# A two-branch encoder layer on one core: attention products trimmed to the query rows that see the keys, exponentials in a slot of their own, first weights staged in idle buffers, and a reordered passage to the tail

## The chip, the core and the metric

The kernel runs on one core of one Trainium2 chip. Its engines work in parallel, each through its own queue in order: TensorE (PE; its weight loads are shown as PEld), VectorE (DVE), ScalarE (ACT), GpSimd (POOL), and SyncE (SP), which here issues all DMAs. The metric is the device time of one execution in microseconds. Before the change it is 2601.07 us, the median of three runs (2600.2 to 2602.27).

## The reference

Two groups of 2048 tokens (prompt and sample) pass through one layer with shared weights. Cut to what matters:

```python
h = rms_norm(x, norm_w)                                    # 1024 wide
q_a, k_a, v_a, g_a, q_b, k_b, v_b, g_b = split(h @ w_in)   # 512,128,128,512, 4 x 512
# A: 8 query heads on 2 key heads, keys within +-128 tokens, a sink per head
o_a = windowed_gqa_sink(rope(norm(q_a)), rope(norm(k_a)), v_a, sink_a) * silu(g_a)
# B: tokens as a grid of 32 rows x 64 columns; row r sees the 8 rows from clip(r - 4, 0, 24),
#    and 16 columns; a learned bias by distance; 8 heads of 64
o_b = neighbourhood_attn(norm(q_b), norm(k_b), v_b, rpb_b) * silu(g_b)
x = x + concat(o_a, o_b) @ w_out
x = x + (p @ w_ple) * sigmoid(x @ w_ple_gate)
```

## The kernel before, in words

Everything is fp32. Each operand of a product is held as a high part (`hi`) and a remainder (`lo`), and a product is three matmuls, hi x hi, hi x lo and lo x hi. A weight is split by `split_w`: ACT casts the high part (L148), DVE subtracts (L149). A tile of x is split by `split`: ACT casts (L295), POOL subtracts (L296). `mm` (L203) records a matmul, `tr` (L206) a transpose, which is a matmul against an identity matrix `ident`.

Work goes over tiles `f` of 128 tokens. **Stage A** takes tiles 0 to 31: per tile the projections `pk` (keys and values), `pq` (queries) and `pg` (gate) of branch A, and an attention unit of an earlier tile. **Stage B** takes tiles 32 to 95, that is each group twice, once for each half of the eight heads: `pqk` and `pvg` project, and a unit of attention works on a query block of 8 grid rows x 16 columns. Such a unit makes four score matrices (`scb`, 128 queries x up to 512 keys), adds the bias and takes the maximum on DVE, takes exponentials on ACT (L233, with the sums of rows in `den`; `nm`, the negated maximum, comes from DVE, L229), transposes them on PE in chunks of up to 128 keys (`ptb`, L206), copies them to `p_t` as hi (ACT, L735) and lo (DVE, L736), and multiplies with the values (`pob`, L203). One `pob` matmul takes a chunk of keys and streams 256 columns, 128 queries in hi and 128 in lo. A unit has 3 or 4 chunks and 4 heads, and there are 832 such matmuls. `fin` transposes the gate (`pgtb`) and multiplies.

PE's order is fixed by hand: a stream of projection matmuls, with pieces of the units set in at the places that the tables `PLAN_A` and `PLAN_B` give, as fractions of the tile's projections. `P(...)` pins an instruction of another engine to its place in the program; what is not pinned is moved by a scheduler. Weights that change between stages are loaded in pieces by jobs that a pump releases, or that `flush` runs by name.

**The head** (tiles 0 and 1) has no earlier tile to fill PE with. `load_first` (L188) brings two row blocks of weights at a time into a staging tile in one of the three `p_t` buffers, and splits them: `wx` for pk, `wa` (w_q) for pq, `wb` (w_g) for pg. Then PE takes pk of both tiles, pq of both and pg of both. pk, pq and pg share the PSUM buffers "pj" (3); score and transpose tiles use "sc" (3).

**The passage to the tail**: the last tiles of `out_ahead` multiply the finished attention outputs with w_out (`pout`), add x (`ev`, L844 to L846) and store. The tail then does the remaining output projection and the gate's by products of sums of blocks, seven products instead of eight for each group of 512 tokens. `load_q` (L952) loads the weight sums `s1` to `s4` (tiles `s`, `wb`), `load_raw` the attention outputs of one group (`oar`, L979, and `obr`, L980), and `prep(m)` makes the operand `opd` of product m (sums at L1009 to L1020, the cast at L995). The products are the matmuls `acca` and `accc` (L1043).

## Time and profile before

| | |
|---|---|
| median of three runs | 2601.07 us |
| the profiled execution | 2597.39 us |
| its span, from the first to the last instruction | 2595.6 us |
| mean granted TensorE clock in it | 0.993 |
| busy share PE / DVE / ACT / POOL | 98% / 75% / 54% / 30% |
| DMA traffic | 357.49 MB, mean 138 GB/s |

A row of a timeline gives the start in us from the span's beginning, the busy us, engine, line, operation, output <- inputs, the shape, how many instructions were merged into the row (x), and in brackets how long the engine stood idle before it and what ended that. PE is the engine that is nearly always busy; so what matters is where it waits and how long its instructions take from start to start, since matmuls overlap and their busy times add to more than they cost. SPq is the queue of SP, and its rows are the issuing of DMAs, not the transfers.

### The profile page before, as it was taken

The numbers are of one execution on the slowest core, as the hardware profiler recorded it, in microseconds if no ns is written. First come the engines' busy times: TensorE is split into PE (matmuls) and PEld (weight loads), VectorE is DVE, ScalarE is ACT, GpSimd is POOL, SyncE is SP. The second block draws the span as 40 slices with busy tenths as digits, with TensorE's granted clock in tenths as the row PEclk, the third lists the DMA queues.
The fourth block names the chain that finished last, engine by engine and source line by source line (L and its number), as shares of the span: only waits on it lengthen the run. The fifth ranks groups of instructions, "written<-read, shape, count | busy, mean of one in ns | idle before, by whom it ended". The sixth has DMA issues, their size and how long they took to land.

```text
span 2595.6 us, 47039 instructions
## 1 busy us (share of the span) xinstructions
PE 2538.2 (98%) x16080; PEld 2273.8 (88%) x16080; DVE 1938.8 (75%) x5702; ACT 1414.0 (54%) x3327; POOL 787.3 (30%) x996
## 2 busy tenths in 40 slices
PE   7999999999989999999999999999989999999999
PEld 5888888888877888888788888888989999999999
DVE  5888888888886888888888888888655648555454
ACT  5666666666664666666766666666432214222222
POOL 3332333332223333333233333321122323233321
PEclk9999999999999999999999999999999999999999
DMA  5333332111143554555654554456575455232221
GB/s 178 108 109 102 108 87 94 60 62 52 62 122 105 183 191 152 183 187 165 219 188 153 187 170 154 151 162 200 172 257 180 154 172 182 82 118 91 78 82 45
DMA packets 227518, 357.49 MB, mean 138 GB/s; under 512 B 37936, under 2 KB 115376, under 8 KB 222128
## 3 DMA queue, kind: packets, MB, share of 16 engines
q1 hardware_dynamic: 227280, 354.50, 42.7%
q8 instruction: 127, 2.08, 0.3%
q14 instruction: 111, 0.91, 0.1%
HBM read 266.33 MB, written 105.92 MB: 143 GB/s over the span
## 4 chain that ended last, share of the span: by engine, by line
PE 89%; DVE 5%; ACT 3%; DMA 2%; issue 1%; POOL 1%; SPq 0%; DVEq 0%; ACTq 0%; POOLq 0%
PE pqk L203 13%; PE pvg L203 12%; PE acca L1043 12%; PE accc L1043 9%; PE pg L203 6%; PE pq L203 6%; PE pob L203 4%; PE pple L203 3%; PE pout L203 3%; PE ptb L206 3%; PE scb L203 3%; PE sc L203 3%; PE pk L203 3%; PE po L203 3%; PE pt L206 3%
## 5 line engine op out<-in xcount | busy, mean ns | idle before, releaser
L233 ACT ACTIVATE s<-s,nm 128x384 f32<-128x384 f32 (+4 forms) x512 | 306.1, 600 | 311.3 <-DVE nm L229 185.0
L203 PE MATMUL pvg<-wb,xr 128*128 128x512 f32 x1536 | 456.7, 405 | 0.0
L203 PE MATMUL pqk<-wa,xr 128*128 128x512 f32 x1536 | 436.6, 407 | 0.0
L203 PEld LDWEIGHTS pqk<-wa,xr 128*128 128x128 f32 x1536 | 266.9, 189 | 37.0
L203 PEld LDWEIGHTS pvg<-wb,xr 128*128 128x128 f32 x1536 | 268.5, 189 | 31.7
L296 POOL TENSOR_TENSOR xr<-stx,xr 128x512 fp32r<-128x512 f32 x192 | 246.6, 1298 | 152.9 <-ACT xr L295 152.5
L203 PE MATMUL pg<-wb,xr 128*128 128x512 f32 x768 | 233.3, 411 | 3.6 <-DVE q L463 3.6
L203 PE MATMUL pq<-wa,xr 128*128 128x512 f32 x768 | 221.9, 402 | 4.1 <-ACT wa L148 2.5
L244 POOL TENSOR_TENSOR g<-qg,rd 128x256 f32<-128x256 f32 x64 | 39.5, 618 | 494.9 <-DVE rd L242 481.0
L1043 PE MATMUL acca<-opd,s 128*128 128x256 f32 x1344 | 166.0, 285 | 3.1 <-ACT r L1075 2.5
L1043 PEld LDWEIGHTS acca<-opd,s 128*128 128x128 f32 x1344 | 164.1, 193 | 3.8 <-ACT r L1075 2.7
L203 PEld LDWEIGHTS pq<-wa,xr 128*128 128x128 f32 x768 | 140.2, 190 | 28.3 <-ACT wa L148 3.0
L218 DVE CUSTOM_DVE_ANT_0 s<-scb,bias 128x288 f32<-128x288 f32 (+3 forms) x256 | 141.8, 555 | 29.1 <-PE scb L203 23.7
L203 PEld LDWEIGHTS pg<-wb,xr 128*128 128x128 f32 x768 | 138.7, 191 | 25.1 <-issue 4.0
L735 ACT CAST p_t<-ptb 96x384 fp32r<-96x384 f32 (+3 forms) x256 | 129.5, 508 | 52.8 <-PE ptb L206 50.9
L736 DVE TENSOR_TENSOR p_t<-ptb,p_t 96x384 fp32r<-96x384 f32 (+3 forms) x256 | 149.0, 584 | 8.2 <-ACT p_t L735 5.3
L616 ACT ACTIVATE ks_b<-pktb,wk 64x128 fp32r<-64x128 f32 x256 | 125.1, 489 | 49.3 <-DVE ks_b L617 41.6
L203 PEld LDWEIGHTS pob<-p_t,vw 128*128 128x128 f32 (+2 forms) x832 | 132.8, 190 | 20.7 <-DVE p_t L736 2.5
L617 DVE SCALAR_TENSOR_TENSOR ks_b<-pktb,wk,ks_b 64x128 fp32r<-64x128 f32 x256 | 115.1, 450 | 38.8 <-ACT ks_b L616 31.7
L203 PE MATMUL pob<-p_t,vw 128*128 128x256 f32 (+2 forms) x832 | 140.5, 282 | 2.0 <-DVE p_t L736 2.0
L1009 POOL TENSOR_TENSOR opd<-sum,opd 128x1024 fp32r<-128x1024 f32 x28 | 69.6, 2484 | 232.1 <-ACT opd L995 232.1
L576 DVE TENSOR_TENSOR pr<-pt,pr 128x512 fp32r<-128x512 f32 x184 | 125.5, 684 | 14.6 <-ACT pr L575 13.6
(197 smaller groups left out, 5870.3 us busy)
## 6 DMA issues: line engine op xcount, KB each, us to landing
stx<-x_b SPq DMA_DIRECT2D x128, 256.0 KB
vw<-v_d SPq DMA_DIRECT2D x112, 256.0 KB
stx<-x_a SPq DMA_DIRECT2D x64, 256.0 KB
stn<-x_n SPq DMA_DIRECT2D x64, 256.0 KB
v_d<-vb SPq DMA_DIRECT2D x64, 256.0 KB
x1r<-x_d SPq DMA_DIRECT2D x16, 1024.0 KB
y_t<-r SPq DMA_DIRECT2D x64, 256.0 KB
v_d<-vb SPq DMA_DIRECT2D x96, 128.0 KB
```

What stands on the lines that cost most here:

```text
L203: pinned(nc.tensor.matmul(out, lhsT, rhs, start=start, stop=stop))
L206: pinned(nc.tensor.transpose(out, in_, ident))
L218: nc.vector.tensor_tensor_reduce(out=s[:, :n], in0=ps[:, :n], in1=bias, scale=1.0, scalar=-3.0e38, op0=ALU.add, op1=ALU.max, accum_out=sm[ ...
L233: nc.scalar.activation(ss[i][:, :n], ss[i][:, :n], AF.Exp, bias=nm[:, i:i + 1], accum_out=den[:, i:i + 1])
L296: nc.gpsimd.tensor_tensor(out=lo, in0=raw, in1=hi.bitcast(F32), op=ALU.subtract)
L576: nc.vector.tensor_tensor(out=pr[:, 1], in0=pf, in1=pr[:, 0].bitcast(F32), op=ALU.subtract)
L616: nc.scalar.activation(hi, pkt[a:a + 64, i], AF.Copy, scale=wk[a:a + 64, 1:2])
L617: nc.vector.scalar_tensor_tensor(out=lo, in0=pkt[a:a + 64, i], scalar=wk[a:a + 64, 1:2], in1=hi.bitcast(F32), op0=ALU.mult, op1=ALU.subtract)
L735: nc.scalar.copy(p_t[:kc, :nch, 0], pf)
L736: nc.vector.tensor_tensor(out=p_t[:kc, :nch, 1], in0=pf, in1=p_t[:kc, :nch, 0].bitcast(F32), op=ALU.subtract)
L1009: each(lambda x, y, z: eng.tensor_tensor(out=x, in0=y, in1=z, op=ALU.subtract), out, a, b)
L1043: pinned(nc.tensor.matmul(ps[:, kk], w[k][:, a, c:c + 128], o[:, b, k], start=i in (0, 1, 4) and kk == 0 and k == 0 and j == 0, stop=k == ...
```

## The change

It has four parts.

1. **Trim.** A grid row of queries sees 8 rows of keys, so in a chunk of 4 or 5 rows of keys part of the 8 query rows see nothing and their probabilities are zero. `query_rows` gives the rows that see chunk j. The transposes go against a permuted identity (`rowwise`), so that the queries come out row by row; chunks are packed in `p_t` with the seen rows only; the `pob` matmuls run over these columns, the chunk with all the rows first. Of the 832 matmuls, 320 keep 256 columns, 256 have 128, 128 have 160 and 128 have 224. The copies to `p_t` shrink with them (128 x 512 to 128 x 368, 120 x 384 to 120 x 288, 384 to 320 or 304 in the others), and the output needs no rearranging in `fin`.
2. **Exponentials.** In stage B `nm` stays at the last score; the four exponentials get a slot of `PLAN_B` of their own (0.16), the first one pinned, in the order in which the transposes take them (0, 2, 1, 3).
3. **Head.** All first weights are loaded at once, into tiles that are idle then (`p_t`, `raw`, `qg`), and split later. The remainder of tile 0's x is made on DVE instead of POOL. pk of tiles 0 and 1 and pg of tile 1 use "sc" for PSUM. The gate splits are pinned behind the first pq. The transposes of tile 0's queries come after 18 of the matmuls of tile 1's pg. The first loads of later tiles come after the weights'.
4. **Passage.** The load of `oar` and `obr` comes ahead of the loads of s2, s1 and s3; the x tiles for the last `ev` are loaded ahead; the `ev` additions and the operands of products 0 to 13 are pinned; the weight jobs are flushed in three places instead of one.

The core of the diff:

```diff
+def query_rows(b, cb, j):
+    r0, _, _, _, rows = window(b, cb)
+    k0 = r0 + rows * j
+    see = [r for r in range(8) if k0 - 7 <= min(max(8 * b + r - 4, 0), 24) <= k0 + rows - 1]
+    return (see[0], max(see[-1] + 1, 4)) if see[0] == 0 else (min(see[0], 4), see[-1] + 1)
...
 PLAN_B = (
...
-    (0.24, 0, "fin", 0), (0.35, 1, "prep", 0),
+    (0.16, 1, "exp", 0), (0.24, 0, "fin", 0), (0.35, 1, "prep", 0),
...
+    nc.gpsimd.tensor_copy(rowwise.rearrange("p (r c) -> p r c", c=16), ident.rearrange("p (c r) -> p r c", r=8))
...
-        for i in range(4):
-            nc.scalar.activation(ss[i][:, :n], ss[i][:, :n], AF.Exp, bias=nm[:, i:i + 1],
-                                 accum_out=den[:, i:i + 1])
+        for n_, i in enumerate((0, 2, 1, 3) if sink is None else range(4)):
+            ex = nc.scalar.activation(ss[i][:, :n], ss[i][:, :n], AF.Exp, bias=nm[:, i:i + 1],
+                                      accum_out=den[:, i:i + 1])
+            if sink is None and n_ == 0:
+                P(ex)
...
+    st = [main.tile([128, 4, 256], F32, tag="p_t", name="ws", bufs=3) for _ in range(2)]
...
+    raws_q += load_first(main.tile([128, 2, 512], F32, tag="p_t", name="ws", bufs=3), 0, 256, 512)
+    raw = ap.tile([128, 4, 512], F32, tag="raw", name="ws", bufs=1)
+    raws_q += load_first(raw[:, 0:2], 2, 256, 512)
...
+        split(0, i, low=nc.vector)
+        for j in range(2 * i, 2 * i + 2):
+            split_w(wx[:, j], raws_x[j], nw[:, j:j + 1])
...
+    for j in (0, 2):
+        raws_g += load_first(main.tile([128, 2, 512], F32, tag="p_t", name="ws", bufs=3), j, 768, 512)
+    for j in range(4, KT):
+        raws_g += load_first(ap.tile([128, 1, 512], F32, tag="qg", name="wg", bufs=6), j, 768, 512)
...
-        pk = ptile([128, 256], "pj", "pk")
+        pk = ptile([128, 256], "pj" if f > 1 else "sc", "pk")
...
-        pg = ptile([128, 512], "pj", "pg")
+        pg = ptile([128, 512], "sc" if f == 1 else "pj", "pg")
...
+        sees = [query_rows(b, cb, j) for j in range(nch)]
+        order = sorted(range(nch), key=lambda j: sees[j][1] - sees[j][0])
+        at = [16 * sum(z - a for a, z in sees[:j]) for j in range(nch + 1)]
...
-            for j in range(nch):
-                tr(pt[:kc, 128 * j:128 * j + 128], sm["s"][h][:, kc * j:kc * j + kc])
+            for j in order:
+                c = at[j] - 16 * sees[j][0]
+                tr(pt[:kc, c:c + 128], sm["s"][h][:, kc * j:kc * j + kc], rowwise)
...
-            for j in range(nch):
-                mm(po[:, i, :], vw[j][:kc, h, :], p_ts[x][:kc, j].rearrange("p a q -> p (a q)"),
-                   j == 0, j == nch - 1)
+            for j in order[::-1]:
+                a, z = sees[j]
+                mm(po[:, i, :].rearrange("p (a q) -> p a q", a=2)[:, :, 16 * a:16 * z], vw[j][:kc, h, :],
+                   p_ts[x][:kc, :, at[j]:at[j + 1]], j == order[-1], j == order[0])
...
-            nc.vector.tensor_tensor(out=ev, in0=ps, in1=ev, op=ALU.add)
+            ev = evs[mp] if evs else load_ev(n, mp)
+            P(nc.vector.tensor_tensor(out=ev, in0=ps, in1=ev, op=ALU.add))
...
+            for j in range(KT // 2, KT):
+                split_w(w[j], raws[j], nw[:, j:j + 1])
+            drain(first[0], 23)
+            for j in range(KT):
+                split_w(w_g[j], raws_g[j], nw[:, j:j + 1], P)
+            drain(first[0], 1)
+            drain(first[1], 24)
+            continue
         for gen in first:
+            if count > 24 and gen is first[1]:
+                drain(gen, 18)
+                nxt(-1)
             drain(gen, count)
...
+        load_o(AHEAD - 1, False)
+        evs = [load_ev(AHEAD - 1, mp) for mp in range(3)]
         load_raw(0)
+        evs.append(load_ev(AHEAD - 1, 3))
+        LEAD = 2
+        ahead = out_ahead(AHEAD - 1, evs)
+        drain(ahead, 24)
+        for name in ("s2", "s1", "s3"):
+            ws[0][name] = load_q(0, name)
         for _ in range(3):
             load_x()
-        flush("0s3")
-        LEAD = 2
-        ahead = out_ahead(AHEAD - 1)
-        drain(ahead, 144)
+        drain(ahead, 120)
         prep(0)
+        flush("0s2")
         drain(ahead)
...
         prep(1)
+        flush("0s1")
...
-            if m == 4:
-                flush("0s4")
+            flush({0: "0s3", 4: "0s4"}.get(m))
```

The order in which the engines issue these things is best seen in three places. First SP's DMAs of the head (`stx` and `stn` are x and the normalised copy of it, `ws` and `wg` staged weights, 128x2x512 is two row blocks of w_q or w_g; `ev` is x for the tail). Before:

```order
L188 DMA ws<-w_in 128x2x256 x3
L278 DMA stx<-x_a 128x512 x2
L278 DMA stn<-x_n 128x512
L188 DMA ws<-w_in 128x2x256
L278 DMA stn<-x_n 128x512
L188 DMA ws<-w_in 128x2x512 x2
L278 DMA stn<-x_n 128x512 x2
L278 DMA stx<-x_a 128x512 x2
L351 DMA snk<-sink 128x8
L354 DMA cs<-rope 128x512
L356 DMA rw<-rope_w 128x64
L188 DMA ws<-w_in 128x2x512 x2
```

and now:

```order
L290 DMA stx<-x_a 128x512
L198 DMA ws<-w_in 128x2x256
L290 DMA stx<-x_a 128x512
L198 DMA ws<-w_in 128x2x256 x3
L290 DMA stx<-x_a 128x512 x2
L198 DMA ws<-w_in 128x2x512 x2
L290 DMA stn<-x_n 128x512 x2
L198 DMA ws<-w_in 128x2x512
L352 DMA cs<-rope 128x512
L354 DMA rw<-rope_w 128x64
L290 DMA stn<-x_n 128x512 x2
L198 DMA ws<-w_in 128x2x512
```

The third and fourth loads of w_q were the last row shown, behind the loads of the normalised x, of a later tile and of three small tables. Now the fourth is the last row shown, the third stands four rows ahead of it, and the loads of later tiles come after this piece.

Second, ACT at the change of halves in stage B (`wa` is the second half's weight, `s,den<-s,nm` the exponentials, `p_t<-ptb` the copy after the transposes; each line number of before has moved down by 11 to 36). Before:

```order
L148 ACTIVATE wa_16591<-wa_16591,nw 128x512
L295 CAST xr<-stx 128x512
L148 ACTIVATE wa_16593<-wa_16593,nw 128x512
L754 COPY otb<-pob 64x512
L148 ACTIVATE wa_16595<-wa_16595,nw 128x512
L148 ACTIVATE wa_16597<-wa_16597,nw 128x512
L148 ACTIVATE wa_16599<-wa_16599,nw 128x512
L689 CAST q1b<-pqtb 64x256
L233 ACTIVATE s,den<-s,nm 128x512 x4
L689 CAST q1b<-pqtb 64x256
L735 CAST p_t<-ptb 128x4x128
```

and now:

```order
L159 ACTIVATE wa_16590<-wa_16590,nw 128x512
L307 CAST xr<-stx 128x512
L159 ACTIVATE wa_16596<-wa_16596,nw 128x512
L790 COPY otb<-pob 64x512
L243 ACTIVATE s,den<-s,nm 128x512 x4
L159 ACTIVATE wa_16598<-wa_16598,nw 128x512
L159 ACTIVATE wa_16600<-wa_16600,nw 128x512
L159 ACTIVATE wa_16602<-wa_16602,nw 128x512
L718 CAST q1b<-pqtb 64x256
L771 CAST p_t<-ptb 128x368
```

Three of the weight casts that stood ahead of the exponentials stand behind them.

Third, DVE in the passage to the tail (`opd<-oar` is the remainder for product 0, `opd<-obr` for product 1, `sum` the sum for product 2, `s_...` the remainders of the weight sums). Before:

```order
L153 TENSOR_TENSOR s_24977<-s_24977 128x512
L153 TENSOR_TENSOR s_24979<-s_24979 128x512
L1009 TENSOR_TENSOR opd<-oar,opd 128x1024
L1009 TENSOR_TENSOR opd<-obr,opd 128x256 x4
L1012 TENSOR_TENSOR sum<-sum,oar 128x1024
L845 TENSOR_TENSOR ev<-pout,ev 128x512 x2
L1070 TENSOR_TENSOR r<-acca,xres 128x512 x2
```

and now:

```order
L1053 TENSOR_TENSOR opd<-oar,opd 128x1024
L164 TENSOR_TENSOR s_25027<-s_25027 128x512
L164 TENSOR_TENSOR s_25029<-s_25029 128x512
L164 TENSOR_TENSOR s_25031<-s_25031 128x512
L164 TENSOR_TENSOR s_25033<-s_25033 128x512
L882 TENSOR_TENSOR ev<-pout,ev 128x512 x2
L1053 TENSOR_TENSOR opd<-obr,opd 128x256 x4
L164 TENSOR_TENSOR s_25035<-s_25035 128x512
L164 TENSOR_TENSOR s_25037<-s_25037 128x512
L164 TENSOR_TENSOR s_25039<-s_25039 128x512
L164 TENSOR_TENSOR s_25041<-s_25041 128x512
L1056 TENSOR_TENSOR sum<-sum,oar 128x1024
```

The additions `ev`, which free the PSUM of `pout`, stood behind all of the first operands and are now ahead of `opd<-obr`; the remainders of the weight sums, which stood ahead of all of these, are spread between them. On SP, `oar` and `obr` stood behind the twelve loads `s<-sums` and are now ahead of them.

117 lines of the change are left out of this document (58 added, 59 removed).

## The prediction

> **What bounds the kernel now.** I read the page first, then busy time by stretches of the span, then PE's timeline wherever a stretch was not full, and at each hole the timeline of the engine that ended it. From the page:
>
> ```profile
> PE 2538.2 (98%) x16080; PEld 2273.8 (88%) x16080; DVE 1938.8 (75%) x5702; ACT 1414.0 (54%) x3327; POOL 787.3 (30%) x996
> PE 89%; DVE 5%; ACT 3%; DMA 2%; issue 1%; POOL 1%; SPq 0%; DVEq 0%; ACTq 0%; POOLq 0%
> ```
>
> PE is busy for 2538.2 of 2595.6 us and is 89% of the chain that ended last. So only two things can be won: matmul time, and the holes in PE's row. The stretches (window, its length, busy us of PE, PEld, DVE, ACT, POOL, the granted clock, DMA share, GB/s) say where the holes are:
>
> ```profile
> 0.00:51.45 51.45, 36.16 (x151) 28.81 (x152) 30.59 (x106) 25.88 (x51) 17.17 (x33) 0.93 0.56 179
> 800.00:1250.00 450.00, 449.55 (x2395) 377.65 (x2395) 357.21 (x1133) 280.17 (x662) 147.27 (x173) 1.00 0.55 175
> 1250.00:1285.00 35.00, 29.02 (x152) 22.68 (x152) 32.09 (x78) 28.61 (x60) 12.15 (x14) 1.00 0.70 224
> 1890.00:1935.00 45.00, 36.12 (x283) 35.36 (x282) 24.98 (x35) 15.10 (x27) 11.67 (x11) 0.92 0.78 261
> 1935.00:2595.60 660.60, 651.97 (x5411) 650.96 (x5410) 373.22 (x484) 182.84 (x275) 193.48 (x112) 1.00 0.36 122
> ```
>
> The steady part of stage B has no hole (449.55 of 450): there an edit counts only if it shortens matmuls. The head lacks 15.3 us of 51.45, the change of halves 6.0 of 35, the passage to the tail 8.9 of 45. The change touches all three.
>
> **The head (tiles 0 and 1).** PE's timeline, then ACT, DVE, SP and the stretch of densest transfers:
>
> ```profile
> 7.06 0.58 PE L203 MATMUL pk<-wx,xr 128*128 128x256 f32 x1 [7.06 <-ACT wx L148]
> 22.96 0.49 PE L203 MATMUL pq<-wa,xr 128*128 128x512 f32 x1 [2.52 <-ACT wa L148]
> 29.05 5.70 PE L203 MATMUL pq<-wa,xr 128*128 128x512 f32 x24 [0.43 <-DVE vr L430]
> 38.40 3.85 PE L203 MATMUL pg<-wb,xr 128*128 128x512 f32 x10 [3.65 <-DVE q L463]
> 51.45 0.76 PE L203 MATMUL pk<-wx,xr 128*128 128x256 f32 x5
> ...
> 4.47 0.62 ACT L295 CAST xr<-stx 128x512 fp32r<-128x512 f32 x1 [2.45 <-DMA stx<-x_a]
> 22.19 2.65 ACT L148 ACTIVATE wa<-ws,nw 128x512 fp32r<-128x512 f32 x4 [2.08 <-DMA ws<-w_in]
> ...
> 7.04 2.89 DVE L149 SCALAR_TENSOR_TENSOR wx<-ws,nw,wx 128x256 fp32r<-128x256 f32 x6 [3.41 <-ACT wx L148]
> 16.80 2.75 DVE L149 SCALAR_TENSOR_TENSOR wa<-ws,nw,wa 128x512 fp32r<-128x512 f32 x4 [2.11 <-ACT wa L148]
> 20.98 1.43 DVE L359 TENSOR_TENSOR tab<-cs,rw 128x256 f32<-128x256 f32 x4 [0.48 <-DMA rw<-rope_w]
> 23.02 0.17 DVE L127 TENSOR_SCALAR rqki<-vr 128x3 int32<-128x3 int32 x1
> 37.58 0.68 DVE L463 TENSOR_TENSOR q<-pq,y 128x512 f32<-128x512 f32 x1
> ...
> 9.36 0.97 SPq L188 DMA_DIRECT2D ws<-w_in  x2
> 17.42 1.20 SPq L188 DMA_DIRECT2D ws<-w_in  x2
> ...
> 17.00:22.00 5.00, 3.15 (x12) 1.94 (x12) 3.94 (x10) 3.11 (x8) 0.00 (x0) 1.00 1.03 357
> ```
>
> The weights come through three staging buffers, so the second half of w_q is issued only at 17.42, once the first half has been split, and PE meets that at 22.96. The gate weights follow through the same buffers, and pg finds a PSUM buffer only at 38.40, after tile 0's q has been read. In the changed order all of w_q is issued without such a wait, and pk and pg of tile 1 stand in other PSUM buffers, so two of the three causes go. What is late next is the last w_q split. By transfers: x of both tiles (1.0 MB), wx (1.0), w_q (2.1), two normalised tiles and the rope table (1.3) are 5.4 MB; at 357 GB/s that takes 15 us from about 1.7 us, hence 17, and at 250 GB/s 23. By DVE, counted from the first x at 5.1 (4.47 + 0.62): two x remainders now moved to it from POOL 2 x 0.68, eight wx at 0.48 = 3.9, eight wa at 0.69 = 5.5, the table 1.43, some 16 small ones at 0.17 = 2.7: 14.9 us, so 20.0 without any waiting. I put 2 us of waiting on top, as DVE stood before in that place, and take 22 for the last w_q split. pq of tile 0 then ends near 23.3. Behind it stand pq of tile 1 and pg of both, each 24 matmuls in 5.70 us: 17.1, and about 0.7 of transposes: 41.1 against 51.45, a gain of 10.3. The eight gate splits (6 us of DVE) must come before pg's last third at about 34; the order puts them at 25 to 33. What is paid back: the transposes of tile 0's q now stand after 18 matmuls of the last pg (at about 39.5), and its rotated q comes from DVE and POOL only at about 38 to 40; 0 to 2.4 us, I take 0.5. The next hole, where the first scores wait for DVE, stays. **Head: -10, from -6 to -13.**
>
> **The trim.** It takes no matmul away. Of the 832 pob matmuls 320 keep 256 columns, 256 fall to 128, 128 to 160, 128 to 224 (52 key chunks over the 16 windows of a group, each met in 2 groups, 2 halves and 4 heads). PE's timeline in stage B:
>
> ```profile
> 1264.40 0.74 PE L203 MATMUL pob<-p_t,vw 128*128 128x256 f32 x4 [2.02 <-DVE p_t L736]
> 1264.98 1.10 PE L203 MATMUL pqk<-wa,xr 128*128 128x512 f32 x4
> ...
> 1500.24 0.51 PE L203 MATMUL pob<-p_t,vw 120*128 120x256 f32 x3
> 1500.59 0.40 PE L203 MATMUL pvg<-wb,xr 128*128 128x512 f32 x1
> 1500.83 0.33 PE L203 MATMUL scb<-ks_b,q1b 128*128 128x360 f32 x1
> 1501.00 0.33 PE L203 MATMUL scb<-ks_b,q 128*128 128x360 f32 x1
> ```
>
> The busy time of one (0.28 us) misleads, since matmuls overlap; starts count. Three pob take 1500.24 to 1500.59, 117 ns each. After an idle array, four take 580 ns until the next product starts (1264.40 to 1264.98): 4 x 117 leaves 112 ns, which is the first weight load with nothing to hide it. A weight load per matmul of about 110 ns is therefore a floor: a trimmed one saves 7 of 117 ns, whatever its width. 512 x 7 = 3.6 us, and I use 4. The two ends: no floor, where a column costs its share of 117 ns (58, 73 and 102 ns remain): 256 x 59 + 128 x 44 + 128 x 15 = 22.6 us; and nothing at all. That the trimmed operand and output are read in two pieces costs nothing: the scb matmul reads 360 columns in 15 pieces in 170 ns (1500.83 to 1501.00), the rate of pob. I take the floor, as a load has been seen alone in this trace. The page "TensorE: Matmul & The Clock Gate" of the Trainium skill, section "LDWEIGHTS (loading the stationary operand)", speaks against this part too: a load takes its columns divided by 1.2 ns, whatever the rows, and by that estimate the 128 columns here take 107 ns and the sum would be 512 x 10 = 5 us. The smaller copies to p_t relieve ACT and DVE, which are not what PE waits for. **Trim: -4, from 0 to -22.**
>
> **The later exponentials.** In a steady unit (ACT's row and the transposes of that window):
>
> ```profile
> 1502.14 0.60 ACT L233 ACTIVATE s<-s,nm 128x360 f32<-128x360 f32 x1 [3.23 <-DVE nm L229]
> L206 PE MATMUL ptb<-ident,s x12: 270/271/273, 1505.7 to 1510.7; 128*120 128x128 f32 x12
> ```
>
> The first exponential starts at 1502.14, as soon as DVE has its bias, and the first transposes come at 1505.7. The new slot lies next to the old one; some 3 us of cover hide it, and if a unit lost that cover each us would cost 64 us over the 64 units. At the change of halves DVE has less between the denominators and p_t, but three weight casts now follow the exponentials on ACT and their remainders go in front of p_t on DVE: of the 2.02 us at 1264.40 I expect about 0.5 back. **-0.5, from -2 to +1.5.**
>
> **The passage to the tail.**
>
> ```profile
> 1900.64 8.44 SPq L952 DMA_DIRECT2D s<-sums  x12
> 1909.90 0.37 SPq L979 DMA_DIRECT2D oar<-oa_d  x1
> 1918.09 1.04 ACT L995 CAST opd<-oar 128x1024 fp32r<-128x1024 f32 x1 [1.98 <-DMA oar<-oa_d]
> 1919.23 0.47 PE L1043 MATMUL acca<-opd,wa 128*128 128x256 f32 x2 [2.27 <-issue]
> 1920.44 2.90 PE L1043 MATMUL acca<-opd,wa 128*128 128x256 f32 x22 [0.74 <-DVE opd L1009]
> 1921.05 3.05 DVE L1009 TENSOR_TENSOR opd<-obr,opd 128x256 fp32r<-128x256 f32 x4 [0.66 <-ACT opd L993]
> 1924.71 3.35 DVE L1012 TENSOR_TENSOR sum<-sum,oar 128x1024 f32<-128x1024 f32 x1 [0.61 <-POOL sum L1009]
> 1927.98 1.27 DVE L845 TENSOR_TENSOR ev<-pout,ev 128x512 f32<-128x512 f32 x2
> 1928.80 4.61 PE L1043 MATMUL acca<-opd,wa 128*128 128x256 f32 x24 [5.46 <-DVE ev L845]
> ...
> L1009 POOL TENSOR_TENSOR opd<-sum,opd 128x1024 fp32r<-128x1024 f32 x28 | 69.6, 2484 | 232.1 <-ACT opd L995 232.1
> ```
>
> SP issues oar behind twelve weight loads (3 MB, 8.44 us), so the first operand is cast only at 1918.09, after the last pout: 2.27 + 0.74 us. Then the additions that free pout's PSUM stand on DVE behind opd and a sum that waits for POOL: 5.46 us. Behind that hole 24 matmuls take 4.61 us where 22 took 2.90: 1.4 us more, the clock. Together 9.9. With oar and obr ahead of the twelve, the first operand is ready long before 1917, and the additions stand ahead of opd<-obr, so these waits go. Late next is the third product's operand. Its chain on DVE after the last pout (1917.0): addition 0.64, opd 3.05 at worst, four weight remainders 2.8 (0.69 each, as for wa), the sum 3.35 at worst, cast 1.04, POOL's remainder 2.48: 1930.3, where two products of 48 matmuls at 117 ns, 11.2 us, let PE arrive at 1928.2. 0 to 2 us remain; I take 1. **Passage: -9, from -5 to -10.** The twelve loads come later themselves: product 1 needs their first four, and they have the pout time in front of it.
>
> **Sum.** -10 - 4 - 0.5 - 9 = -23.5 us. Span 2595.6 to 2572; with the 1.8 us around it, the profiled 2597.39 to 2574. The median of the runs shown is 3.7 above that profiled run, so 2601.07 - 23.5 = 2577.5 us.
>
> **Rivals.**
> (a) No load floor: the trim brings 22.6, 19 more: 2559. For it: weights load beside a running matmul here all the time; against it: the 112 ns.
> (b) The head gives a third only: DVE carries the x remainders and sixteen splits and is the bound; if each split waits for its ACT cast as at 16.80 (2.11 us) and the q transposes stall the full 2.4, -4 remains: 2583.5. For it: the rows of 16.80 to 37.58 show DVE with this work in front of pg before too; against it: the first splits no longer wait for transfers.
> (c) The jam on DVE at the passage returns one product later: four weight remainders stand in front of the sum, and they need their loads. If these land at 1925, product 2 waits 5: 2582.5.
> (d) Slower: ACT is in order, and the first exponential is now fixed in its place. Were an otb copy or a cast ahead of it to wait for PE, p_t would be late in each of the 64 units, as it is at 1264.40 (2.02 us). It decides from 23.5 / 64 = 0.37 us a unit; at 0.6 us the time is 2616. Against it: the 3 us of cover.
>
> **How the numbers follow.** The sum as told 0.55, (a) 0.08, (b) 0.17, (c) 0.15, (d) 0.05. Likeliest 2577.5; its own terms alone span about 2570 to 2586. (b) and (c) lie inside 2562 to 2589, which leaves out (a), (d) and the two together, under 2 in 10. A change under 0.2% (5.2 us) can't be told from none here; that needs (b), (c) and no trim at once: 0.05. Slower is (d) and a remainder: 0.05. Faster 0.90.
>
> **What would show it.** In the changed profile: pk of tile 2 starts near 41 and the last w_q split ends near 22 (if at 26 or later, (b)); starts of three trimmed pob lie 110 ns apart (if 60 to 70, (a); if 117 or more, no trim); the first exponential of a unit ends before the first transpose with PE still full between 800 and 1250; the first acca follows the last pout without a hole, and the clock stays at 1.00 there (if a hole of several us stands before the third product, (c)). Wrong would be holes in stage B that were not there.

## The result, and the profile after

The changed kernel takes 2585.64 us (median of four runs, 2584.15 to 2590.74); the kernel before, measured beside it, 2600.64 (four runs, 2599.71 to 2602.27). The ratio is 0.9942, with a 95% interval of 0.9930 to 0.9954: 15 us faster, between 12 and 18. The forecast of 2577.5 had the sign right and 8.5 us too much of it; 2585.64 lies inside its range.

The profiled execution took 2586.14 us, its span 2584.1. The one of before (2597.39) lay 3.25 below this median of 2600.64, and this one 0.5 above its own, so the two traces differ by only 11.3 to 11.5 us. The account below is made of the traces and comes to 11.35. Of the page, the busy times and the shares of the chain of waits:

```profile
PE 2531.9 (98%) x16080; PEld 2268.0 (88%) x16080; DVE 1922.3 (74%) x5704; ACT 1392.3 (54%) x3327; POOL 792.2 (31%) x995
PE 85%; DVE 8%; ACT 3%; issue 2%; DMA 2%; POOL 1%; SPq 0%; DVEq 0%; ACTq 0%; POOLq 0%
```

PE's share of the chain fell from 89 to 85%, DVE's rose from 5 to 8%: the span is shorter, but more of it is waiting for DVE. The stretches (columns as in the prediction; the windows are shifted to the same work):

```profile
0.00:43.42 43.42, 33.41 (x150) 27.42 (x151) 32.25 (x105) 25.67 (x52) 11.81 (x29) 0.96 0.62 218
790.00:1240.00 450.00, 446.79 (x2389) 374.13 (x2390) 348.32 (x1138) 272.46 (x662) 148.14 (x173) 1.00 0.56 173
...
1880.00:1925.00 45.00, 44.08 (x369) 43.88 (x368) 25.99 (x36) 15.16 (x28) 11.79 (x10) 1.00 0.94 318
1925.00:2584.10 659.10, 645.14 (x5349) 643.61 (x5348) 377.49 (x485) 182.44 (x275) 199.77 (x114) 1.00 0.36 119
```

The head lacks 10.0 us of PE instead of 15.3, and the passage 0.9 of 45 instead of 8.9. Two stretches are worse: stage B, which was full, lacks 3.2 us in 450, and the tail behind 1925 lacks 14.0 where the stretch of before from 1935 lacked 8.6.

Where the same work starts in both traces gives the balance. Each line is the difference, after minus before, in the time from one mark to the next, worked out from the starts in PE's timelines:

```
start of the span to a steady tile of stage A         -9.6
stage A (all of it in one place, near 363 us)         +2.8
change from stage A to B                              +0.1
stage B, from 817 us to the first pout                +2.55
first pout to the second group of the tail (2055)     -5.75
the rest of the tail                                  -1.4
sum                                                  -11.35
```

Inside the fifth line the gain was larger for a while: the third product starts 17.4 us earlier than before in the trace, and by 1962 the lead is down to 11.2. The fifth line is not all the passage: 2.6 of its 5.75 us come before the last pout. Behind a hole of 3 to 3.5 us among the first pout the granted clock is 0.50, in the kernel before for some 8 us (1790 to 1798), in the changed one for some 4 (1786 to 1790). From the first to the last pout the kernels below come out anywhere between +0.8 and -3.0, the one without the new passage at -2.0. From the last pout to 2055 the changed kernel gains 3.2. The last line is a step near 2190, behind a hole of 2.5 us that both kernels have: the granted clock behind it is 0.66 over 5 us in the kernel before and 1.00 in the changed one. Among the kernels below, two more have this step (1.5 us) and ten have 0 to 0.2, so I count it as chance.

### The profile page after: what moved, and what is told of

Read it like the earlier page. It is cut to its first block, busy times and chain, and to the rows that moved or that the text cites. A ratio compares the mean times of both kernels' runs of the same rounds, so it can differ in the third digit from the quotient of the medians.

```text
span 2584.1 us, 47172 instructions
## 1 busy us (share of the span) xinstructions
PE 2531.9 (98%) x16080; PEld 2268.0 (88%) x16080; DVE 1922.3 (74%) x5704; ACT 1392.3 (54%) x3327; POOL 792.2 (31%) x995
## 4 chain that ended last, share of the span: by engine, by line
PE 85%; DVE 8%; ACT 3%; issue 2%; DMA 2%; POOL 1%; SPq 0%; DVEq 0%; ACTq 0%; POOLq 0%
PE pqk L212 12%; PE pvg L212 12%; PE acca L1087 11%; PE accc L1087 8%; PE pq L212 6%; PE pg L212 6%; PE pple L212 4%; PE pout L212 3%; PE ptb L215 3%; PE pk L212 3%; PE scb L212 3%; PE pob L212 3%; PE sc L212 3%; PE po L212 3%; PE pt L215 3%
## 5 line engine op out<-in xcount | busy, mean ns | idle before, releaser
L212 PE MATMUL pqk<-wa,xr 128*128 128x512 f32 x1536 | 444.0, 411 | 0.0
L798 POOL TENSOR_TENSOR o_tb<-otb 128x256 f32<-128x256 f32 x64 | 48.9, 763 | 559.4 <-DVE otb L791 469.8
L227 DVE CUSTOM_DVE_ANT_0 s<-scb,bias 128x288 f32<-128x288 f32 (+3 forms) x256 | 141.5, 553 | 21.0 <-PE scb L212 18.5
L772 DVE TENSOR_TENSOR p_t<-ptb,p_t 128x368 fp32r<-128x368 f32 (+5 forms) x256 | 125.2, 490 | 18.4 <-ACT p_t L771 11.1
L215 PE MATMUL ptb<-rowwise,s 128*128 128x128 f32 (+2 forms) x832 | 133.4, 274 | 3.7 <-ACT s L243 3.7
L605 DVE TENSOR_TENSOR pr<-pt,pr 128x512 fp32r<-128x512 f32 x184 | 125.3, 684 | 14.9 <-ACT pr L604 13.9
L227 DVE CUSTOM_DVE_ANT_0 s<-sc,mask 128x384 f32<-128x384 f32 (+1 forms) x256 | 132.6, 537 | 3.1 <-PE sc L212 0.7
```

The source lines that it names most:

```text
L212: pinned(nc.tensor.matmul(out, lhsT, rhs, start=start, stop=stop))
L215: pinned(nc.tensor.transpose(out, in_, eye))
L227: nc.vector.tensor_tensor_reduce(out=s[:, :n], in0=ps[:, :n], in1=bias, scale=1.0, scalar=-3.0e38, op0=ALU.add, op1=ALU.max, accum_out=sm[ ...
L605: nc.vector.tensor_tensor(out=pr[:, 1], in0=pf, in1=pr[:, 0].bitcast(F32), op=ALU.subtract)
L772: nc.vector.tensor_tensor(out=lo, in0=pf, in1=hi.bitcast(F32), op=ALU.subtract)
L798: nc.gpsimd.tensor_tensor(out=o_t, in0=got["ot"][:, :, 0], in1=got["ot"][:, :, 1], op=ALU.add)
```

## The experiments

Each of the twelve starts from the changed kernel. Times of one call stand beside the same runs of the kernel before. "Stage B" below is the difference to before from the first steady product at 817 us to the first pout, the line that is +2.55 above.

### One part undone at a time

The trim off (every chunk is taken to be seen by all rows; the row-by-row order and all else stay):

```diff
-        sees = [query_rows(b, cb, j) for j in range(nch)]
+        sees = [(0, 8)] * nch
```

> The changed kernel, but all pob matmuls again with 256 columns (every chunk is taken as seen by all 8 query rows; permuted transposes and packing stay). Theory, a weight load is the floor: in the changed kernel three pob with 160 or 128 columns start 67 to 74 ns apart, but the projection behind them takes 270 to 286 ns instead of 231 to 241, so a pair of trimmed matmuls saves only 12 to 15 ns: this kernel is 3 to 4 us longer than the changed one over stage B, and its projections behind pob are back at 231 to 241 ns. Rival, the trimmed matmuls stream freely (the pob starts alone became 14 us shorter): 14 us longer. Rival, the trim brings nothing: the same within 1 us.

The later exponentials off:

```diff
-    (0.16, 1, "exp", 0), (0.24, 0, "fin", 0), (0.35, 1, "prep", 0),
+    (0.24, 0, "fin", 0), (0.35, 1, "prep", 0),
...
-            yield
...
-        for n_, i in enumerate((0, 2, 1, 3) if sink is None else range(4)):
+        for n_, i in enumerate(range(4)):
...
-            if sink is None and n_ == 0:
-                P(ex)
```

> The changed kernel, but the exponentials of stage B again right at the last score, in the order 0, 1, 2, 3 and not pinned. Theory, their later place costs at the change of halves: the start of the first pqk behind it, which came 1.8 us later against its surroundings in the changed kernel, comes 1 to 2 us earlier, and the whole is 1 to 3 us shorter than the changed kernel. Rival, they are covered everywhere and the loss at the change of halves is the weight transfers' or chance: the same within 0.7 us there. Rival, the new slot helps in the steady units: 1 us or more longer.

The head off (all of its hunks undone: weights through three staging buffers, their order, the PSUM buffers, the x remainder on POOL):

```diff
-    def load_first(st, j, c, n):
+    def load_first(j0, w, src):
+        n = w[0].shape[-1]
+        st = main.tile([128, 2, 512], F32, tag="p_t", name="ws", bufs=3)
+        nc.sync.dma_start(st[:, :, :n], src.rearrange("(j p) c -> p j c", p=128))
+        for i in range(2):
+            split_w(w[i], st[:, i, :n], nw[:, j0 + i:j0 + i + 1])
...
```

> The changed kernel with the head of before (first weights through three buffers, x remainders on POOL, PSUM buffers as before). Theory: pk of tile 2 starts at 51 to 52 us instead of 43.4, and the steady stage A runs 9 to 10 us later than in the changed kernel. The changed kernel loses 2.8 us near 363 us, where ACT waits for a transfer behind the store of 4-byte pieces: if that is a consequence of the earlier head, it is not there and the whole is 6.8 us longer than the changed kernel; if it is chance of the transfers, it is there in some runs of either and the whole is 9 to 10 us longer.

The passage off (the order of the loads, the x tiles loaded ahead, the pins, the three flushes):

```diff
-            P(nc.vector.tensor_tensor(out=ev, in0=ps, in1=ev, op=ALU.add))
+            nc.vector.tensor_tensor(out=ev, in0=ps, in1=ev, op=ALU.add)
...
-            pin = P if m < 14 else lambda ins: ins
...
+        flush("0s3")
+        LEAD = 2
+        ahead = out_ahead(AHEAD - 1)
+        drain(ahead, 144)
```

> The changed kernel with the passage to the tail of before (oar and obr behind the twelve weight sums, additions behind the first operands). Theory: the third product starts 13 us later than in the changed kernel counted from the first pout, and the give-back in the following four products (6.2 us) goes too, so the whole is 7 us longer. Rival, the give-back has nothing to do with the new order: 13 us longer.

And both parts of stage B off, which are the first two edits together:

> The changed kernel with both the trim and the later exponentials undone (permuted transposes and packing stay), that is, the new head and the new passage on the old stage B. By the starts of the first products, from the first pqk of stage B's steady part to the first pout, the changed kernel lost 2.6 to 2.9 us against before, the one without the trim 1.9, the one without the later exponentials 5.9. Theory, each of the two edits shifts waits in stage B and both together cost: here this stretch is as long as before within 0.7 us, and the whole 2 to 3 us shorter than the changed kernel. Rival, the loss is in the permuted transposes and the packing, which this kernel keeps: the stretch stays 2 us or more longer than before.

Measured:

```
                          median   ratio to before (95%)      stage B   first pout to 2177   last pout to 2177
changed kernel           2585.64   0.9942 (0.9930 to 0.9954)   +2.55        -5.7                -3.1
trim off                 2586.98   0.9956 (0.9942 to 0.9971)   +1.87        -3.85               -3.2
exponentials off         2589.61   0.9964 (0.9953 to 0.9976)   +5.9         -4.84               -3.4
head off                 2597.07   0.9990 (0.9981 to 0.9999)   +2.89        -6.1                -3.2
passage off              2586.28   0.9954 (0.9939 to 0.9969)   +2.88        -3.47               -1.5
trim, exponentials off   2586.26   0.9953 (0.9935 to 0.9970)   +0.69        -3.44               -3.2
```

In the medians only the head's row is clear of the changed kernel's; exponentials off just touches it, and the others overlap it. The columns to the right come from one trace each. How well they repeat can be seen where the code is the same: stage B is +2.55 to +2.94 in six kernels, and the last column is -3.1 to -3.4 in seven of the eight kernels with this passage (-2.3 in the eighth). The column from the first pout does not repeat (-3.44 to -6.1 with the same passage), for the slow clock told above.

Several expectations were missed. Without the trim, stage B was to be 3 to 4 us longer and is 0.7 shorter. Without the later exponentials the whole was to be 1 to 3 us shorter and is 4 longer, which had been named as a rival. Without the passage 7 us were expected, and 0.6 came. Without both parts of stage B that stretch came as expected, 0.69 (and 0.55 in a second kernel below), so the permuted transposes and the packing, which stay in it, are not the loss; the whole, expected 2 to 3 us shorter, is not shorter.

**The head is most of the gain.** Without it 2.6 us of the 15 remain (0.1% of 2600). In the eleven traced variants with the new head and in the changed kernel, the lead at a steady tile of stage A is 8.0 to 11.5 us, median 9.4; without it the kernel is 0.7 behind there.

**Stage B does not gain.** By the traces it is 0.7 slower than before with both of its parts undone, 2.55 with both, and 5.9 with the trim alone. Why the trim brings so little is seen in the groups of PE from 817 to 1888 us (busy us, mean ns of one | idle before). In the changed kernel:

```profile
L212 PE MATMUL pvg<-wb,xr 128*128 128x512 f32 x1437 | 433.7, 408 | 0.0
L212 PE MATMUL pqk<-wa,xr 128*128 128x512 f32 x1416 | 410.5, 412 | 0.0
...
L212 PE MATMUL pob<-p_t,vw 128*128 128x256 f32 (+7 forms) x832 | 126.4, 265 | 3.6 <-DVE q L719 3.3 <-DVE p_t L772 0.3
```

and with the trim off:

```profile
L212 PE MATMUL pvg<-wb,xr 128*128 128x512 f32 x1423 | 424.9, 404 | 0.0
L212 PE MATMUL pqk<-wa,xr 128*128 128x512 f32 x1416 | 404.0, 408 | 0.0
L212 PE MATMUL pob<-p_t,vw 128*128 128x256 f32 (+2 forms) x832 | 140.5, 282 | 2.9 <-DVE q L719 2.9
...
```

The trimmed pob are 14.1 us less busy in sum, but every projection became 4 ns longer, and 4 ns x 2853 is 11.4 us. It isn't every one: sorted by what stands ahead, only a projection that follows a pob changed. From start to start, in us, from the first pqk to the first pout (740 pob and 228 projections right behind one; a hole is what goes beyond 0.5 us; the remaining matmuls, 190 to 192 us in each, are left out of the lines but not of the last):

```
                               before   trim off   both off   exp. off    changed
pob                             86.87      87.24      87.03      73.77      75.03
pqk and pvg behind a pob        55.18      54.99      55.20      65.06      65.05
other pqk and pvg              696.07     696.47     695.44     700.24     696.97
holes                            9.49      10.61       9.42      12.34      12.19
all                           1037.91    1040.12    1038.08    1043.51    1040.18
```

A projection behind a pob took 241 ns (55 us / 228) and takes 285. So a short matmul hands its time on: while it streams, the 128 columns of the next projection's weights must load, and the projection waits for them. Against the kernel with the same exponentials the trim is worth 12.2 - 10.1 = 2.1 us (trim off to changed), against the one without them 13.3 - 9.9 = 3.4. Its price is in the next two lines of the table: the holes grow by 1.6 and 2.9, and in the trim alone the other projections by 4.8, which includes waits shorter than 0.5 us. They are of this kind (the trim alone, PE's timeline):

```profile
1451.84 0.44 PE L215 MATMUL pktb<-ident,kb 128*128 128x128 f32 x2 [0.20 <-DVE otb L788]
```

Over the units the time from the last pvg to this transpose of the keys is 15.7 us in sum with both parts off and 19.7 with the trim alone; in 12 units it is 0.35 us longer each. PE comes there earlier, and DVE has not yet freed the PSUM buffer. The later exponentials take these waits away (the sum is 14.9 in the changed kernel). They are worth 3.3 us with the trim (1043.51 to 1040.18) and cost 2.0 without it (1038.08 to 1040.12). The two parts belong together, and together they still cost 2 in the traces (the medians, 2585.64 and 2586.26, do not show it).

### The trim with half of the weights

To tell the weight load from the other explanations, I measured pob with 64 weight columns instead of 128, once trimmed and once not (the product with the other half of the values is left out, so these two kernels do not compute the layer):

```diff
-                mm(po[:, i, :].rearrange("p (a q) -> p a q", a=2)[:, :, 16 * a:16 * z], vw[j][:kc, h, :],
+                mm(po[:64, i, :].rearrange("p (a q) -> p a q", a=2)[:, :, 16 * a:16 * z], vw[j][:kc, h, :64],
...
-                nc.scalar.copy(ot[a:a + 64], pq[z:z + 64])
-                nc.vector.tensor_tensor(out=ot[a:a + 64], in0=pq[a:a + 64], in1=ot[a:a + 64], op=ALU.add)
+                nc.scalar.copy(ot[a:a + 64], pq[0:64])
+                nc.vector.tensor_tensor(out=ot[a:a + 64], in0=ot[a:a + 64], in1=ot[a:a + 64], op=ALU.add)
```

The second of the two also has the first experiment's edit.

> A cost measured by itself: the changed kernel, but each pob matmul loads only 64 of the 128 weight columns; the product with the other part of the values is left out, and the additions behind it add the first part to itself. Theory, the weight load (about 110 ns for 128 columns) is the floor: with half the columns the projection behind trimmed pob takes 231 to 245 ns as behind full ones, and a run of three or four pob with the matmul behind it is 40 to 110 ns shorter than in the kernel with half the weights and no trim. Rival, the projection behind short matmuls is held up by something else (the switching of PSUM, the fetch of instructions): it still takes 266 to 287 ns.

> The counterpart: the same half of the weight columns (the other part of the values left out as there), but all pob matmuls with 256 columns. Theory: pob 117 ns apart, the projection behind them 231 to 243 ns as before, so that its runs are those of before, and the trimmed counterpart is 40 to 110 ns shorter per run; over 256 runs that is 15 to 22 us of matmul time, less what waits take back. Rival: the runs of both differ by 8 to 16 ns as with whole weights.

One run of each: 2577.82 trimmed, 2584.78 not. The trim that is worth nothing clear with whole weights is worth 7.0 us here; two single runs of one kernel can differ by that much (2579.20 and 2587.19 below), but the traces say 6.0 from the first pqk to the first pout (1040.80 to 1034.78). A run of four pob and what follows, in PE's timeline (a merged row shows the form of its first matmul). Trimmed with whole weights, the changed kernel:

```profile
1457.57 0.56 PE L212 MATMUL pob<-p_t,vw 128*128 128x256 f32 x4
1457.97 1.61 PE L212 MATMUL pqk<-wa,xr 128*128 128x512 f32 x6
```

whole weights, the trim off:

```profile
1454.50 0.63 PE L212 MATMUL pob<-p_t,vw 128*128 128x256 f32 x4
1454.96 1.55 PE L212 MATMUL pqk<-wa,xr 128*128 128x512 f32 x6
```

half weights, trimmed:

```profile
1450.09 0.51 PE L212 MATMUL pob<-p_t,vw 128*64 128x256 f32 x4
1450.43 1.60 PE L212 MATMUL pqk<-wa,xr 128*128 128x512 f32 x6
```

and half weights, not trimmed:

```profile
1454.19 0.63 PE L212 MATMUL pob<-p_t,vw 128*64 128x256 f32 x4
1454.66 1.55 PE L212 MATMUL pqk<-wa,xr 128*128 128x512 f32 x6
```

The four starts before the pqk are 118, 100, 70 and 110 ns apart in the first, 116, 118, 116 and 114 in the second, 119, 102, 61 and 62 in the third and 117, 117, 116 and 114 in the fourth; the pqk behind takes 293, 232, 280 and 232. The whole runs take 691, 696, 624 and 696 ns: the trim wins 5 ns with whole weights and 72 with half. With half of the columns to load, two trimmed pob in a row stream at 61 ns, and untrimmed ones gain nothing: the weight load is the floor for short matmuls, and only for them. What I expected of the projection behind was wrong: it does not return to 232, since it has 128 columns of its own to load. In sums from the first pqk to the first pout, the half weights' pob fall by 18.5 us (87.05 to 68.60), the projections behind rise by 10.7 as they do with whole ones. The page "TensorE: Matmul & The Clock Gate" of the Trainium skill, section "LDWEIGHTS (loading the stationary operand)", makes a load its columns divided by 1.2 ns, by which estimate 128 take 107 ns and 64 take 53. The trace agrees to within 10 ns: 61 and 62 for 64 columns, and for 128 columns 110 in the third run (62, and the 48 by which the pqk behind exceeds 232) and 115 in the first (118, 100, 70, 110 and 61, by four; its single starts are uneven, only their sum says this).

### The change of halves

The changed kernel's timeline of PE there:

```profile
1260.00 0.67 PE L212 MATMUL pob<-p_t,vw 128*128 128x256 f32 x4 [3.26 <-DVE q L719]
1260.50 1.15 PE L212 MATMUL pqk<-wa,xr 128*128 128x512 f32 x4
```

The hole of 2.02 us grew to 3.26, and DVE's `q` ends it, which reads pqtb out of a PSUM buffer of the kind that pob needs ("ms", 1259.51 to 1259.94); p_t is ready at 1259.01. The test moved the exponentials of the two units at that place ahead of the casts again:

```diff
+                if f in (57, 58):
+                    next(got["ex"])
...
-        return {..., "exp": lambda _: next(got["ex"])}
+        return {..., "exp": lambda _: f in (57, 58) or next(got["ex"])}
```

> The changed kernel, but in the two units at the change of halves the exponentials are issued right at the last score, so that the three weight casts no longer stand between them and the copies to p_t as now. Theory, those casts and their remainders in front of p_t on DVE are the 1.8 us lost there: the hole before pob at the change of halves falls from 3.4 to about 2.1 us and the following pqk comes 1 to 2 us earlier against its surroundings. Rival, the loss comes from what feeds the weights: no change there.

Measured 2584.47 (2583.57 to 2586.01), ratio 0.9942 (0.9926 to 0.9958). Its timeline of PE:

```profile
1257.36 1.03 PE L212 MATMUL pob<-p_t,vw 128*128 128x256 f32 x4 [1.99 <-DVE q L719]
1258.19 2.02 PE L212 MATMUL pqk<-wa,xr 128*128 128x512 f32 x4
...
1268.27 0.50 PE L212 MATMUL scb<-ks_b,q1b 128*128 128x512 f32 x1 [0.77 <-DVE mx L227]
```

The hole is 1.99, as expected. The four pqk behind it take 2.02 us instead of 1.15, but that is no new loss: the granted clock is 0.55 and 0.53 from 1257.3 to 1261 here and 0.50 from 1262 to 1264 in the changed kernel, and from the end of the hole to the first scb both take the same (6.72 and 6.75 us). What is new is a wait of 0.77 for the maximum. Over the whole place (1208 to 1282 us of before) it loses 1.64 us against before where the changed kernel loses 1.83 (five other kernels with the same code there 2.0 to 2.25), and the kernel with both parts of stage B undone 1.02. The exponentials are the cause of the longer hole; moving them back moves most of the loss on to the next wait.

### The passage

PE in the changed kernel, then DVE, POOL, ACT and SP:

```profile
1910.06 5.92 PE L1087 MATMUL acca<-opd,wa 128*128 128x256 f32 x48
1915.82 5.92 PE L1087 MATMUL accc<-opd,wa 128*128 128x256 f32 x48
1921.58 5.92 PE L1087 MATMUL acca<-opd,s 128*128 128x256 f32 x48
1928.23 5.99 PE L1087 MATMUL acca<-opd,s 128*128 128x256 f32 x48 [0.73 <-DVE r L1114]
...
1943.64 7.48 PE L1087 MATMUL accc<-opd,wb 128*128 128x256 f32 x48 [3.67 <-DVE r L1124]
...
1917.55 7.60 DVE L164 TENSOR_TENSOR s<-s 128x512 fp32r<-128x512 f32 x4 [0.51 <-ACT s L163]
...
1937.92 1.22 DVE L1053 TENSOR_TENSOR opd<-sum,opd 128x1024 fp32r<-128x1024 f32 x1 [0.59 <-ACT opd L1068]
1939.06 1.42 DVE L1053 TENSOR_TENSOR opd<-obr,opd 128x256 fp32r<-128x256 f32 x4
1940.40 2.49 DVE L164 TENSOR_TENSOR wb<-wb 128x512 fp32r<-128x512 f32 x4
1942.81 1.28 DVE L1124 TENSOR_TENSOR r<-accc,r 128x512 f32<-128x512 f32 x2
...
1922.25 5.22 POOL L1053 TENSOR_TENSOR sum<-obr,oar 128x256 f32<-128x256 f32 x4
...
1900.37 1.05 ACT L1068 CAST opd<-oar 128x1024 fp32r<-128x1024 f32 x1 [12.98 <-DVE ev L882]
...
1894.97 0.37 SPq L1021 DMA_DIRECT2D oar<-oa_d  x1
```

The load comes 15 us earlier than before and the first operand is cast at 1900.37 instead of 1918.09; three products follow one another without a hole. The price comes three products on. The matmul at 1943.64 adds into the PSUM that `r<-accc` must read first, and that read is queued on DVE behind 5 us of work; the hole is 3.67. The work is the remainder of this product's own operand (`opd<-sum`, 1.22), that of the next product's (`opd<-obr`, 1.42) and the four weight remainders of s4 (2.49). Only the first is needed here; the steps of the tail (L981) take a22 for this product, number 5, and s4 for number 6, and the tiles of both are named `wb`. Behind the hole the granted clock is 0.62 (1943.6 to 1946) and 0.80 (1946 to 1950), so the 48 matmuls take 7.48 us instead of 5.92. A second hole of 1.35 follows at 1987, in the next group of products. From the last pout to the third product the trace gains 10.69 us against before, the same in every kernel with the new passage, and 4.79 without it; up to 2032 it then gives 7.5 back (0.7, 3.7, 1.6 for the slow clock and 1.5, in the main), 3.3 without it.

The first two ideas were that the remainders are late (s3) or in the way (s4). Earlier s3:

```diff
         flush("0s1")
+        flush("0s3")
...
-            flush({0: "0s3", 4: "0s4"}.get(m))
+            flush({4: "0s4"}.get(m))
```

> The changed kernel, but the last four of the twelve weight sums (s3) are split right behind s1, ahead of the operand of product 2, instead of behind it. In the changed kernel their four remainders take 7.6 us on DVE (1.9 each) because POOL works on its sums at the same time, where the first eight took 0.62 to 0.68 each. Theory, this slowing makes DVE late for the additions behind the following products: here they take 2.7 us, and the hole before the first accc with wb (3.8 us) falls under 1 us; the passage gains 3 to 5 us. Rival, the hole comes from the split of s4, pinned ahead of the two additions that free its PSUM: the hole stays at 3 us or more, and product 2 starts up to 1 us later.

and s4 one product earlier:

```diff
-            flush({0: "0s3", 4: "0s4"}.get(m))
+            flush({0: "0s3", 3: "0s4"}.get(m))
```

> The changed kernel, but the weight sums s4 are split one product earlier, so that on DVE their four remainders (2.5 us) stand ahead of the operand opd<-obr of the product after next. The two additions that free the PSUM stay behind all of these. Theory of the slowed remainders: no change of the hole of 3.8 us, since the work ahead of the additions is the same. Rival, the place of the s4 split decides: the hole shrinks by 1.4 us or more.

Measured 2582.75 (2579.20 to 2587.19), ratio 0.9936 (0.9919 to 0.9952), and 2585.14 (2583.91 to 2587.03), 0.9945 (0.9927 to 0.9963). The hole stays in both. With s3 early, PE and DVE:

```profile
1942.04 4.18 PE L1087 MATMUL accc<-opd,wb 128*128 128x256 f32 x18 [3.08 <-DVE r L1124]
...
1911.95 4.90 DVE L164 TENSOR_TENSOR s<-s 128x512 fp32r<-128x512 f32 x8
```

With s4 early, PE:

```profile
1940.79 3.54 PE L1087 MATMUL accc<-opd,wb 128*128 128x256 f32 x15 [3.66 <-DVE r L1124]
```

In the one, DVE is done with the remainders early, but the read still stands behind the same opd and wb rows. In the other only their order changed. Both ideas fell. What is left is the order itself: s4 behind the read, and no pins from product 6 on:

```diff
-            pin = P if m < 14 else lambda ins: ins
+            pin = P if m < 6 else lambda ins: ins
...
-            flush({0: "0s3", 4: "0s4"}.get(m))
+            flush({0: "0s3", 5: "0s4"}.get(m))
```

> The changed kernel, but the weight sums s4 are split one product later (behind the additions of the product that the hole of 3.8 us follows) and only the operands of products 0 to 5 are pinned, not 0 to 13. Both earlier ideas on that hole failed (it stayed at 3.2 and 3.8 us). New theory: the matmul that waits adds to the PSUM that DVE must read first, and that reading (r<-accc) is queued behind pinned work for later products, 2.5 us of s4's remainders and 1.4 us of the next operand: the hole falls under 1 us, the hole of 1.5 us of the same kind one group later goes too, and the passage gains 4 to 5.5 us against the changed kernel. Rival, DVE is simply full there: the hole moves behind the next product and the gain stays under 1.5 us.

Measured 2582.29 (2580.81 to 2584.80), ratio 0.9938 (0.9925 to 0.9952). PE and DVE:

```profile
1940.14 5.99 PE L1087 MATMUL accc<-opd,wb 128*128 128x256 f32 x48 [2.58 <-ACT wb L163]
...
1932.23 1.23 DVE L1056 TENSOR_TENSOR sum<-sum,oar 128x1024 f32<-128x1024 f32 x1 [1.32 <-POOL sum L1053]
...
1937.51 1.22 DVE L1053 TENSOR_TENSOR opd<-sum,opd 128x1024 fp32r<-128x1024 f32 x1
1938.64 0.75 DVE L1053 TENSOR_TENSOR opd<-obr,opd 128x256 fp32r<-128x256 f32 x2
1939.32 1.28 DVE L1124 TENSOR_TENSOR r<-accc,r 128x512 f32<-128x512 f32 x2
```

The wait is 2.58 us long, where under 1 was expected. The profile puts it down to ACT's cast of wb, but that is s4, which this product does not use; the first of the two reads ends at 1940.0, 0.14 us ahead of the matmul, as it ends 0.15 ahead of it in the changed kernel. So it is still the read. The weight remainders are out of its way, but the scheduler, no longer bound by pins, has put a sum of product 9 (L1056, at 1932.23, which first waits 1.32 us for POOL) ahead of the sums of this product's operand. Without that sum and its wait, 2.5 us, the hole would be near 0.1 (an estimate from these rows; it was not tried). The queue did hold PE: the hole is 1.1 us shorter, the granted clock behind it stays at 1.00 (5.99 us for the 48 instead of 7.48), and the hole of one group later is gone. From the last pout to 2177 us the trace gains 7.3 us instead of 3.1 (4 to 5.5 more were expected), and between the third product and the second group 3.4 us are given back instead of 7.5. In the timed runs the two intervals overlap; faster than the changed kernel is not shown. The same edit with both parts of stage B undone:

> The new head and passage with that mended tail, on the old stage B (trim and later exponentials undone; permuted transposes and packing stay). Theory: from the steady part of stage B to the first pout 2 us less than the changed kernel, the passage 4 to 5.5 us less: 6 to 7.5 us shorter than the changed kernel, 20 to 23 us shorter than before (ratio about 0.992), if the head gains its 8 to 11 us. Rival, the mended tail only moves the hole: 2 to 3 us shorter than the changed kernel.

gave 2582.63 (2581.73 to 2583.85), ratio 0.9938 (0.9924 to 0.9951): the same time. In its trace stage B is +0.55, and from the last pout to 2177 us it gains 7.2 us, so that gain repeats. The 6 to 7.5 us expected against the changed kernel did not come; the medians differ by 3.0, and faster is not shown here either.

Undoing the passage costs less than the 9 us forecast, 1.7 us of the trace (-1.5 against -3.1 from the last pout) and nothing clear in the medians. One reason is the jam; the other stands in its PE and DVE rows:

```profile
1911.05 0.77 PE L1083 MATMUL acca<-opd,wa 128*128 128x256 f32 x2 [2.26 <-issue]
1912.26 8.19 PE L1083 MATMUL acca<-opd,wa 128*128 128x256 f32 x46 [0.44 <-DVE opd L1049]
...
1912.12 0.68 DVE L877 TENSOR_TENSOR ev<-pout,ev 128x512 f32<-128x512 f32 x1
1912.87 3.42 DVE L1049 TENSOR_TENSOR opd<-obr,opd 128x256 fp32r<-128x256 f32 x4
```

The wait of 2.26 us for the late load is back, but not the one of 5.46 us: with the other parts in, the scheduler itself puts an `ev` addition ahead of `opd<-obr`, though the code of the passage is that of before. The largest of the waits that the passage was to remove went with a side effect of the others.

### What the loss near 363 us is

Stage A, which no edit touches, loses 2.8 us in one place. ACT and SP of the changed kernel:

```profile
360.58 0.63 ACT L321 ACTIVATE stn<-stn 128x512 f32<-128x512 f32 x1 [5.95 <-DMA stn<-x_n]
...
345.11 1.51 SPq L290 DMA_DIRECT2D stn<-x_n  x1
```

and ACT in the kernel before:

```profile
367.47 0.63 ACT L309 ACTIVATE stn<-stn 128x512 f32<-128x512 f32 x1 [3.26 <-DMA stn<-x_n]
```

A load of x issued at 345.11 lands 15 us later, ACT waits 5.95 us for it instead of 3.26, and PE 2.47 us for DVE behind that. The other kernels lose 0 to 0.9 there. With the same stage A in all of them, I take it for chance of the transfers in this one execution; what delays that load in all of them was not tried.

## Why the prediction was right or wrong

**The bound.** PE, its holes and its matmul time, held as the frame: every line of the balance is one of the two. What it left out, but for the 1.4 us of the passage, is that matmul time also grows behind a hole, by the granted clock.

**Head: -10 forecast, -9.6 measured** (8.0 to 11.5 over the variants), in part by luck. pk of tile 2 starts at 43.42, not 41.1, so only 8.0 us are won up to there. Another 1.4 come at the next hole, where the first scores wait for DVE and of which the prediction said that it stays. PE in the changed kernel:

```profile
20.41 0.96 PE L212 MATMUL pq<-wa,xr 128*128 128x512 f32 x3 [1.16 <-DVE wa L160]
23.00 8.21 PE L212 MATMUL pq<-wa,xr 128*128 128x512 f32 x29 [1.63 <-DVE wa L160]
...
41.55 0.66 PE L215 MATMUL pqt<-ident,q 128*128 128x128 f32 x4 [0.52 <-POOL q L454]
43.42 3.04 PE L212 MATMUL pk<-wx,xr 128*128 128x256 f32 x24
...
48.75 0.50 PE L212 MATMUL sc<-ks_a,q 128*128 128x256 f32 x2 [0.40 <-DVE mx L227]
```

and before:

```profile
57.96 0.51 PE L203 MATMUL sc<-ks_a,q 128*128 128x256 f32 x2 [1.61 <-DVE mx L218]
```

The last w_q split lies at 23 to 24 instead of 22, and DVE ends the two holes, as worked out. Behind the second the granted clock is 0.50 (23 to 25 us) and 0.77 (25 to 27), which the sum did not have, and pq of tile 0 gives way to tile 1's at 25.3 instead of 23.3. The wait for tile 0's rotated q is 0.52, where 0.5 was taken. pg runs behind pq without its 3.65 us. Rival (b), a third of the gain, is excluded.

**Trim: -4 forecast, -2.1 to -3.4 measured for the matmuls themselves.** The floor was there, and rival (a), 22.6 us, was not. The prediction put it in the wrong matmul: it expected trimmed pob 110 ns apart, and by median they are 67 to 111, by their width, with the missing time in the projection behind. By the sign I had named (60 to 70 apart means no floor) a reader would have chosen (a) wrongly; the sum over a run of pob and the next start is what counts. What failed is the sentence that smaller copies "are not what PE waits for", so that the trim could cost nothing: PE arrives earlier at waits for DVE and ACT that were just covered, and the holes took 1.6 to 2.9 us back, in the trim alone another 4 with the short waits ahead of the key transposes.

**Later exponentials: -0.5 forecast.** At the change of halves the hole grew by 1.2 us instead of shrinking by 0.5. The step that failed is the one at that place: I let the casts move behind the exponentials, had their remainders only in front of p_t, and left out that DVE's `q`, behind p_t, must free a PSUM buffer for pob. In the steady units the cover held for PE's transposes to within a few tenths of a us in sum, so (d), the slow case, did not come, but their worth of 3.3 us beside the trim I had not seen either. The sign that the prediction named for being wrong, holes in stage B that were not there, came (3.2 us in 450). Stage B as a whole: -4.5 forecast, +2.55 measured, 7 of the 12 us by which the trace's -11.35 misses -23.5.

**Passage: -9 forecast, -5.75 measured to 2055, of which -3.2 lie behind the last pout.** All three waits named are gone, the clock stays at 1.00 (row 1880.00:1925.00), and the third product starts 10.7 us nearer to the last pout, where 9.9 were worked out. Then the jam came, as rival (c) had it, a queue on DVE in front of something that PE needs; I had looked for it at product 2 and gave it 2582.5, but it stands at product 5, behind pinned work for product 6, and costs 7.5 us with the small hole before it, the slow matmuls and the second hole behind it. The step "0 to 2 us remain" looked one product ahead only. The forecast also took the whole wait of 5.46 us as the edit's own, and without the edit it is gone in the new order too: undoing the passage shows it worth 1.7 us.

**The sum.** Terms measured in the trace: -9.6 + 2.55 - 5.75 = -12.8 against -23.5; the 2.8 lost and 1.4 won by what I take for chance make -11.35, with 0.1 at the change of stages. The medians say -15, since the profiled execution of before lay 3.25 below the median measured beside it; the forecast had carried such an offset (3.7) over to the changed kernel, whose profiled execution lies 0.5 above its own. That the medians miss the forecast by 8.1 us and the traces by 12 is this offset, not a better sum. Faster came, as the 0.90 had it; (c), given 0.15, came in another place.
